# Three weight chunks at the opening of MLP, attention input and FFN: split one after another, or half by half

## The chip, the cores and the metric

The kernel runs on one core of a Trainium2 chip. The metric is device time in microseconds (us) of one execution. Three executions of the kernel before took 2520.97, 2524.18 and 2525.96 us; their median is 2524.18 us.

## What is computed

Two transformer blocks in float32, one after the other, on one sequence of 256 tokens with 2048 channels. Cut to the parts that matter here (both blocks modulate their norms by vectors made from a small input `c`):

```
# block 1: conv mixer, then an MLP
mod = silu(c) @ mod_w + mod_b                 # sh1, sc1, g1, sh2, sc2, g2
x = x + (1 + g1) * conv_mixer(rms_norm(x, norm1_g) * (1 + sc1) + sh1)
h = rms_norm(x, norm2_g) * (1 + sc2) + sh2
x = x + (1 + g2) * (square(relu(h @ mlp_w1)) @ mlp_w2)            # 2048 -> 8192 -> 2048
# block 2: two kinds of attention, then a gated FFN
h = rms_norm(x, norm1_w) * (1 + sc1) + sh1
qa, ka, va, qb, kb, vb, ga, gb = split(h @ w_in)                  # attention input
x = x + g1 * (merged_attention(...) @ w_out)
h = rms_norm(x, norm2_w) * (1 + sc2) + sh2
x = x + g2 * ((silu(h @ w_gate) * (h @ w_up)) @ w_down)           # 2048 -> 5632 -> 2048
return rms_norm(x, final_w)
```

## The kernel before

**Layout.** Activations lie channels first: 16 blocks of 128 channels on the partitions, 256 tokens along the free side. A weight matrix comes in chunks of 1 MB: 128 output channels by 2048 inputs, so a chunk is a tile `wf` of 128 x (16 x 128).

**Float32 by parts.** Each weight chunk and each activation is split into a high part (a cast to fp32r) and a low part (the remainder). A product is three matmuls per block of 128 inputs (`mm`, L189): high weight by high and by low activation, and low weight by high activation. A chunk is therefore 16 x 3 = 48 matmuls. `load_w` (L166) makes the two parts of a chunk in two halves of eight input blocks: for each half a cast by ScalarE into a tile `wh` (L177), then a subtraction by VectorE into a tile `wl` (L180). There are 4 buffers for `wf`, 4 for `wh` and 4 for `wl`, so all split halves that are alive at a time are at most four.

**Order of loads.** `weights` (L136) lists all chunks in the order of use. `take` (L160) returns the next one and always loads and splits one chunk further ahead (AHEAD = 1), so the chunk after the one in use is split before it is needed.

**The stages.** `linear` (L200) walks over the chunks of a matrix. At the opening of a stage whose activations are being made (MLP, attention input, FFN) it takes three chunks at once (`lead=3`): `mm_group` goes over the 16 input blocks and for each of them runs the matmuls of all three chunks, so that TensorE has three chunks' work for each activation block that arrives. All other chunks come one by one. Called w0, w1, w2 here are the three chunks of an opening, and w3, w4 the two that follow. The third `take` of an opening loads and splits w3.

**The norm ahead of a stage.** `norm_to` makes the activations `hHL` of a stage from `x`: for each of the 16 blocks a scaling by VectorE (L342), the high part by ScalarE (L344) and the low part by VectorE (L345). It starts when `rstd` (L302 to L307) has the reciprocal root of the sum of squares, for which TensorE adds up the squares (L327, L329). Ahead of the MLP it also needs the shift vector `SH2` of block 1. That comes from `mod_part_pe`: 16 loads `wm` of 1 MB from `mod_w` (L249), each multiplied by TensorE (L251), then a transpose (L258) and an addition (L259). The `wm` loads use the same 4 `wf` buffers as the weight chunks.

**What sets the order.** The framework's scheduler turns the program into one list for each engine before the run, and gives out the buffers of a pool in the order of the program. Each engine works through its own list. All loads are issued by SyncE (SP).

Of the kernel before, what the change touches and what calls it, by code (L numbers as in the profile page):

```python
# [10 lines left out]
F32R = mybir.dt.float32r  # L11
AF = mybir.ActivationFunctionType
ALU = mybir.AluOpType
AX = mybir.AxisListType

P = 128
D = 2048
KB = D // P
S = 256
# [31 lines left out]
QKV_ORDER = [8, 9, 10, 11, *range(8)] + [b + i for i in range(8) for b in (12, 20, 28)]  # L51
# [21 lines left out]
class Builder:  # L73
# [62 lines left out]
    def weights(self):  # L136

        a = self.a
        out = []
        for j in range(EARLY, 16):  # L140
            out += [(a["conv_in"][16 + j], 16, j not in NATIVE), (a["conv_in"][j], 16)]
        out += [(a["conv_out"][j], 16) for j in range(16)]
        for g in range(4):
            out += [(a["w1"][g * 16 + j], 16) for j in range(16)]
            out += [(a["w2"][j][:, g * D:(g + 1) * D], 16) for j in range(16)]
        out += [(a["win"][b], 16) for b in QKV_ORDER]
        out += [(a["win"][b], 16) for b in (36, 52)]
        for j in range(16):
            if j < 15:
                out += [(a["win"][b + j + 1], 16) for b in (36, 52)]  # L150
            out.append((a["oab"][j], 16))
        out += [(a["wout"][j], 16) for j in range(16)]
        f0 = 0
        for n in FF_GROUPS:
            out += [((a["wg"] if j % 2 == 0 else a["wu"])[f0 + j // 2], 16) for j in range(2 * n)]
            out += [(a["wd"][j][:, f0 * P:(f0 + n) * P], n) for j in range(16)]
            f0 += n
        return out

    def take(self):  # L160
# [2 lines left out]
            self.ahead.append(self.load_w(*self.plan.pop(0)))  # L163
        return self.ahead.pop(0)

    def load_w(self, src, nk=16, parted=True):  # L166

        w = self.wp.tile([P, nk, P], F32, tag="wf", name=self.nm("wf"))
        self.nc.sync.dma_start(out=w, in_=src.rearrange("p (k c) -> p k c", c=P))
        if not parted:  # L170
            return w
        parts = []
        for k0 in range(0, nk, 8):
            n = min(8, nk - k0)
            wh = self.sp.tile([P, n, P], F32R, tag="wh", name=self.nm("wh"))
            wl = self.sp.tile([P, n, P], F32R, tag="wl", name=self.nm("wl"))
            self.nc.scalar.copy(wh, w[:, k0:k0 + n, :])  # L177
            if self.between:
                self.between()
            self.nc.vector.tensor_tensor(out=wl, in0=w[:, k0:k0 + n, :], in1=wh, op=ALU.subtract)  # L180
            parts.append((wh, wl))
        return parts

    def mm(self, ps, w, k, x, first, last):

# [5 lines left out]
    def mm_group(self, ws, x, ks, xs=None):  # L191
# [5 lines left out]
                self.mm(ps, w, k, x[:, kx], i == 0, i == len(ks) - 1)  # L197
        return pss

    def linear(self, n, x, nk, evict, step=None, lead=3):  # L200

        j = 0
        while j < n:
            g = lead if j == 0 else 1
            g = min(g, n - j)
            ws = [self.take() for i in range(g)]
            pss = self.mm_group(ws, x, list(range(nk)))
            for i in range(g):
                evict(j + i, pss[i])
                if step:  # L210
                    step()
            j += g
# [59 lines left out]
    def step(self, n=None):  # L272
        self.due += self.rate if n is None else n
        while self.due >= 1 and self.jobs:
            self.due -= 1
            while self.jobs:
                try:
                    next(self.jobs[0])
                    break
                except StopIteration:  # L280
                    self.jobs.pop(0)
        if not self.jobs:
            self.due = 0.0
# [802 lines left out]
```

## Time and profile before

| | before |
|---|---|
| median of three executions | 2524.18 us (2520.97 to 2525.96) |
| the profiled execution | 2528.09 us |
| its span in the profile | 2526.3 us |
| TensorE busy (matmuls) | 2458.1 us, 97% |
| VectorE, ScalarE, GpSimd busy | 1680.5, 1226.7, 148.7 us |
| moved by DMA | 639.15 MB, mean 253 GB/s |

PE is TensorE's matmuls and PEld its weight loads; DVE is VectorE, ACT ScalarE, POOL GpSimd, SP SyncE. Matmuls are pipelined, so the time of one row is longer than the distance from one to the next. A row's bracket names the idle time of the engine just before it and what ended that. PEclk is the granted TensorE clock as a share of 2.4 GHz: 0.5 is 1.2 GHz.

### The profile page before, as it was taken

How to read it: one execution, taken by the hardware profiler on the slowest of the kernel's cores; microseconds unless marked ns; L12 is line 12 of the kernel's file. 1: busy time of each engine (PE TensorE's matmuls, PEld its weight loads, DVE VectorE, ACT ScalarE, POOL GpSimd, SP SyncE). 2: the span in 40 equal slices, each digit the busy share in tenths (PEclk: the TensorE clock that was granted, in tenths of full speed). 3: DMA queues.
4: the chain of work that ended last, by engine and by line, in shares of the span. 5: the costliest groups of instructions: out<-in, count | busy, mean ns of one | idle time of the engine just before them, and what ended most of it. 6: DMA issues, size and time to landing. Idle time of an engine off the chain costs nothing. (4 is left out here: it accounts for less than half of the span.)

```text
span 2526.3 us, 49401 instructions
## 1 busy us (share of the span) xinstructions
PE 2458.1 (97%) x21100; PEld 2353.7 (93%) x21100; DVE 1680.5 (67%) x2156; ACT 1226.7 (49%) x1827; POOL 148.7 (6%) x184
## 2 busy tenths in 40 slices
PE   6999899999999999999999999999999999999998
PEld 4788678899999999998999999999899999999997
DVE  3477854677777788757876667776666556566555
ACT  3366754554543544544455544444544444434443
POOL 0058900000000000000000000000000000000000
PEclk8999999999999999999999999999999999999999
DMA  9967569788787887954755577775466656665553
GB/s 397 418 237 283 215 265 332 259 306 323 272 324 286 307 326 289 330 187 168 233 193 193 198 270 271 275 290 199 167 221 237 238 206 246 213 236 207 200 181 120
DMA packets 110381, 639.15 MB, mean 253 GB/s; under 512 B 16336, under 2 KB 16592, under 8 KB 51792
## 3 DMA queue, kind: packets, MB, share of 16 engines
q1 hardware_dynamic: 110160, 635.99, 68.8%
q8 instruction: 165, 2.70, 0.4%
q14 instruction: 56, 0.46, 0.1%
HBM read 633.85 MB, written 2.10 MB: 252 GB/s over the span
## 5 line engine op out<-in xcount | busy, mean ns | idle before, releaser
L177 ACT CAST wh<-wf 128x1024 fp32r<-128x1024 f32 (+1 forms) x794 | 827.5, 1045 | 1046.9 <-PE mm L189 791.0
L189 PE MATMUL mm<-hHL,wh 128*128 128x256 f32 x7584 | 1316.5, 278 | 8.1 <-ACT hHL L344 7.7
L180 DVE TENSOR_TENSOR wl<-wf,wh 128x1024 fp32r<-128x1024 f32 (+1 forms) x794 | 965.7, 1222 | 501.7 <-ACT wh L177 497.0
L189 PEld LDWEIGHTS mm<-hHL,wh 128*128 128x128 f32 x7584 | 1151.4, 189 | 19.9 <-ACT hHL L344 9.1
L189 PE MATMUL mm<-hHL,wl 128*128 128x256 f32 x3792 | 1048.8, 277 | 2.1 <-DVE wl L180 2.1
L189 PE MATMUL mm<-uHL,wh 128*128 128x256 f32 x4480 | 768.6, 276 | 1.4 <-ACT uHL L132 0.8
L189 PEld LDWEIGHTS mm<-hHL,wl 128*128 128x128 f32 x3792 | 714.7, 188 | 3.2 <-DVE wl L180 2.9
L189 PEld LDWEIGHTS mm<-uHL,wh 128*128 128x128 f32 x4480 | 675.3, 188 | 14.6 <-ACT t L792 9.2
L189 PE MATMUL mm<-uHL,wl 128*128 128x256 f32 x2240 | 617.4, 276 | 0.0
L189 PEld LDWEIGHTS mm<-uHL,wl 128*128 128x128 f32 x2240 | 420.7, 188 | 0.9 <-issue 0.8
L230 DVE SCALAR_TENSOR_TENSOR acc<-wm,silu_c,acc 128x1024 f32<-128x1024 f32 x210 | 269.4, 1283 | 101.7 <-DMA wm<-in_w_ada_dram 77.6
L623 POOL TENSOR_TENSOR room<-room,front 128x255 f32<-128x255 f32 (+9 forms) x180 | 148.5, 826 | 169.2 <-ACT front L622 156.0
L633 DVE SCALAR_TENSOR_TENSOR mm<-room,vecs,mm 128x255 f32<-128x255 f32 (+9 forms) x180 | 84.7, 470 | 4.8
L189 PE MATMUL mm<-m,wh 128*128 128x256 f32 x512 | 87.6, 276 | 0.0
L622 ACT ACTIVATE front<-room,vecs 128x255 f32<-128x255 f32 (+9 forms) x180 | 74.9, 487 | 8.6 <-POOL room L623 8.4
L189 PEld LDWEIGHTS mm<-m,wh 128*128 128x128 f32 x512 | 77.1, 188 | 0.0
L189 PE MATMUL mm<-m,wl 128*128 128x256 f32 x256 | 70.5, 276 | 0.0
L541 PE MATMUL mm<-hHL,wh 128*128 128x256 f32 x320 | 62.4, 296 | 3.4 <-ACT hHL L132 3.4
L541 PEld LDWEIGHTS mm<-hHL,wh 128*128 128x128 f32 x320 | 52.1, 201 | 10.5 <-issue 6.7
L133 DVE TENSOR_TENSOR uHL<-t,uHL 128x256 fp32r<-128x256 f32 x124 | 51.4, 420 | 3.4 <-ACT uHL L132 3.4
L251 PE MATMUL aux<-wm,cpad 128*32 128x512 f32 x384 | 50.8, 612 | 2.8 <-DMA wm<-in_mod_w_dram 2.7
L132 ACT CAST uHL<-t 128x256 fp32r<-128x256 f32 x124 | 49.3, 403 | 4.6 <-DVE t L953 2.6
(162 smaller groups left out, 1196.0 us busy)
## 6 DMA issues: line engine op xcount, KB each, us to landing
wf<-in_w_dram SPq DMA_DIRECT2D x128, 1024.0 KB, 6.8
wm<-in_w_ada_dram SPq DMA_DIRECT2D x96, 1024.0 KB, 5.7
wf<-in_win_dram SPq DMA_DIRECT2D x68, 1024.0 KB, 5.2
wm<-in_mod_w_dram SPq DMA_DIRECT2D x64, 1024.0 KB, 6.7
wf<-in_wg_dram SPq DMA_DIRECT2D x44, 1024.0 KB, 4.8
wf<-in_wu_dram SPq DMA_DIRECT2D x44, 1024.0 KB, 4.8
wf<-in_wd_dram SPq DMA_DIRECT2D x32, 896.0 KB, 4.6
slots<-in_mod_a_dram SPq DMA_DIRECT2D x22, 1024.0 KB, 15.1
```

What stands on the lines that cost most here:

```text
L132: self.nc.scalar.copy(hi, src)
L133: self.nc.vector.tensor_tensor(out=lo, in0=src, in1=hi, op=ALU.subtract)
L177: self.nc.scalar.copy(wh, w[:, k0:k0 + n, :])
L180: self.nc.vector.tensor_tensor(out=wl, in0=w[:, k0:k0 + n, :], in1=wh, op=ALU.subtract)
L189: self.nc.tensor.matmul(ps, lhsT=a, rhs=x[:, b], start=(first and i == 0), stop=(last and i == 2))
L230: nc.vector.scalar_tensor_tensor(out=acc, in0=w[:, i], scalar=cvec[:, k + i:k + i + 1], in1=acc, op0=ALU.mult, op1=ALU.add)
L251: nc.tensor.matmul(row[32 * j:32 * j + 32, :], lhsT=cpad[:, k], rhs=w[:, j * 512:(j + 1) * 512], start=(k == 0), stop=(k == KB - 1), skip_ ...
L541: nc.tensor.matmul(dst, lhsT=w[:, c, kk], rhs=h[:, k, b], start=(k == 0 and n == 0 and half == 0), stop=(k == KB - 1 and n == 2 and half = ...
L622: nc.scalar.activation(pr, u[:, PAD:PAD + S - s], AF.Identity, scale=tap(i, j))
L623: nc.gpsimd.tensor_tensor(out=dst[:, s:], in0=dst[:, s:], in1=pr, op=ALU.add)
L633: nc.vector.scalar_tensor_tensor(out=acc[:, s:], in0=u[:, PAD:PAD + S - s], scalar=tap(i, j), in1=acc[:, s:], op0=ALU.mult, op1=ALU.add)
```

## The change

`w0`, `w1` and `w2` of the three openings are loaded without being split (a third entry in the list says so: False for them, true for all others). `linear` sees that and calls the new `by_halves`: it splits the first halves of all three chunks, runs the matmuls of input blocks 0 to 7 of all three, then does the same with the second halves. The splitting code itself moves from `load_w` into `parts`. The number of loads, casts, subtractions and matmuls stays as it was. w3 keeps its place in the list: it is loaded and split by the third `take`, ahead of `by_halves`.

```diff
         for g in range(4):
-            out += [(a["w1"][g * 16 + j], 16) for j in range(16)]
+            out += [(a["w1"][g * 16 + j], 16, g > 0 or j > 2) for j in range(16)]
             out += [(a["w2"][j][:, g * D:(g + 1) * D], 16) for j in range(16)]
-        out += [(a["win"][b], 16) for b in QKV_ORDER]
+        out += [(a["win"][b], 16, i > 2) for i, b in enumerate(QKV_ORDER)]
...
-            out += [((a["wg"] if j % 2 == 0 else a["wu"])[f0 + j // 2], 16) for j in range(2 * n)]
+            out += [((a["wg"] if j % 2 == 0 else a["wu"])[f0 + j // 2], 16, f0 > 0 or j > 2) for j in range(2 * n)]
...
+    def parts(self, w, k0, n):
+
+        wh = self.sp.tile([P, n, P], F32R, tag="wh", name=self.nm("wh"))
+        wl = self.sp.tile([P, n, P], F32R, tag="wl", name=self.nm("wl"))
+        self.nc.scalar.copy(wh, w[:, k0:k0 + n, :])
+        if self.between:
+            self.between()
+        self.nc.vector.tensor_tensor(out=wl, in0=w[:, k0:k0 + n, :], in1=wh, op=ALU.subtract)
+        return wh, wl
...
     def load_w(self, src, nk=16, parted=True):
...
         if not parted:
             return w
-        parts = []
-        for k0 in range(0, nk, 8):
-            n = min(8, nk - k0)
...
-            parts.append((wh, wl))
-        return parts
+        return [self.parts(w, k0, min(8, nk - k0)) for k0 in range(0, nk, 8)]
...
+    def by_halves(self, ws, x):
+
+        pss = [self.mmps()[:, :S] for _ in ws]
+        for k0 in (0, 8):
+            halves = [self.parts(w, k0, 8) for w in ws]
+            for k in range(k0, k0 + 8):
+                for ps, part in zip(pss, halves):
+                    self.mm(ps, {k // 8: part}, k, x[:, k], k == 0, k == KB - 1)
+        return pss
+
     def linear(self, n, x, nk, evict, step=None, lead=3):
...
             ws = [self.take() for i in range(g)]
-            pss = self.mm_group(ws, x, list(range(nk)))
+            if g > 1 and not isinstance(ws[0], list):
+                pss = self.by_halves(ws, x)
+            else:
+                pss = self.mm_group(ws, x, list(range(nk)))
```

What the change moves on the engines, at three places. In the list of the changed kernel the lines stand some further down: the cast is L170, the subtraction L173, the activation of the norm L357 (L344 before), the load of a chunk L179 (L169), of `wm` L262 (L249), the matmul still L189.

**Order 1, ScalarE at the opening of the MLP.** Before, w0 is `wf_4488` and w1 `wf_4671`; the rows run from the end of the conv output to the first activation of the norm, and the first cast of w1 comes after eight activations:

```order
L177 CAST wh_4490<-wf_4488 128x1024
L323 ACTIVATE t_466_4478<-x 128x256
L177 CAST wh_4494<-wf_4488 128x1024
L792 ACTIVATE t_474_4547<-mm_4498,vecs 128x256
L323 ACTIVATE t_475_4550<-x 128x256
L302 ACT_TABLE_LOAD
L302 ACTIVATE t_485_4595<-aux_3417,eps 128x256
L255 COPY t_481_4583<-aux_3835 128x512
L344 ACTIVATE hHL_4593<-t_488_4603,mods 128x256
```

In the change w0 is `wf_4488`, w1 `wf_4663`, w2 `wf_4665` and w3 `wf_4667`; the first two rows here are the 13th and the 14th activation of the norm:

```order
L357 ACTIVATE hHL_4585<-t_496_4643,mods 128x256
L357 ACTIVATE hHL_4585<-t_497_4647,mods 128x256
L170 CAST wh_4669<-wf_4667 128x1024
L170 CAST wh_4673<-wf_4667 128x1024
L357 ACTIVATE hHL_4585<-t_498_4651,mods 128x256
L357 ACTIVATE hHL_4585<-t_499_4655,mods 128x256
L170 CAST wh_4680<-wf_4488 128x1024
L170 CAST wh_4684<-wf_4663 128x1024
L170 CAST wh_4688<-wf_4665 128x1024
L170 CAST wh_4764<-wf_4488 128x1024
```

The two casts of w0 stood ahead of the norm; now its first cast stands behind all 16 activations and both casts of w3.

**Order 2, SyncE's loads ahead of the MLP, with the engines and load queues that each waits for.** Before (w0, five pieces of `mod_w` for `SH2`, w1, w2, w3):

```order
L169 DMA wf_4488<-in_w_dram 128x2048 [waits DMAHW3_49,DVE_49]
L249 DMA wm_4553<-in_mod_w_dram 128x2048 [waits DMAHW4_49,PE_49]
L249 DMA wm_4559<-in_mod_w_dram 128x2048 [waits DMAHW5_49,DVE_49]
L249 DMA wm_4565<-in_mod_w_dram 128x2048 [waits DMAHW6_49,PE_49]
L249 DMA wm_4571<-in_mod_w_dram 128x2048 [waits DMAHW7_49,DVE_49]
L249 DMA wm_4577<-in_mod_w_dram 128x2048 [waits DMAHW0_49,PE_49]
L169 DMA wf_4671<-in_w_dram 128x2048 [waits DMAHW1_49,PE_49]
L169 DMA wf_4681<-in_w_dram 128x2048 [waits DMAHW2_49,PE_49]
L169 DMA wf_4691<-in_w_dram 128x2048 [waits DMAHW3_49,PE_49]
```

In the change:

```order
L179 DMA wf_4488<-in_w_dram 128x2048 [waits DMAHW3_49,DVE_49]
L262 DMA wm_4545<-in_mod_w_dram 128x2048 [waits DMAHW4_49,PE_49]
L262 DMA wm_4551<-in_mod_w_dram 128x2048 [waits DMAHW5_49,DVE_49]
L262 DMA wm_4557<-in_mod_w_dram 128x2048 [waits DMAHW6_49,PE_49]
L262 DMA wm_4563<-in_mod_w_dram 128x2048 [waits DMAHW0_49,PE_49]
L262 DMA wm_4569<-in_mod_w_dram 128x2048 [waits DMAHW1_49,PE_49]
L179 DMA wf_4663<-in_w_dram 128x2048 [waits DMAHW2_49,PE_49]
L179 DMA wf_4665<-in_w_dram 128x2048 [waits DMAHW3_49,PE_49]
L179 DMA wf_4667<-in_w_dram 128x2048 [waits DMAHW7_49,DMAHW4_49,PE_49]
```

The order of the loads is the same, but the fourth piece of `mod_w`, which waited for VectorE (it got w0's buffer after the split), now waits for TensorE, and what follows moves one buffer on.

**Order 3, ScalarE and TensorE at the opening of the FFN.** ScalarE before, from w0 (`wf_20194`) and w1 (`wf_20336`) to the first activation of the norm:

```order
L177 CAST wh_20196<-wf_20194 128x1024
L177 CAST wh_20200<-wf_20194 128x1024
L323 ACTIVATE t_2478_20190<-x 128x256
L177 CAST wh_20338<-wf_20336 128x1024
L177 CAST wh_20342<-wf_20336 128x1024
L323 ACTIVATE t_2485_20254<-x 128x256
L302 ACTIVATE t_2488_20261<-aux_19248,eps 128x256
L344 ACTIVATE hHL_20259<-t_2491_20269,mods 128x256
```

In the change, with w3 `wf_20332`, w0 `wf_20194` and w1 `wf_20328`:

```order
L336 ACTIVATE t_2478_20190<-x 128x256
L170 CAST wh_20334<-wf_20332 128x1024
L170 CAST wh_20338<-wf_20332 128x1024
L170 CAST wh_20345<-wf_20194 128x1024
L170 CAST wh_20349<-wf_20328 128x1024
L336 ACTIVATE t_2481_20246<-x 128x256
L315 ACTIVATE t_2484_20253<-aux_19248,eps 128x256
L357 ACTIVATE hHL_20251<-t_2487_20261,mods 128x256
```

TensorE in the change, behind the 48 matmuls of the first halves of w0 and w1 (`mm_20344` is the result of w2, `mm_20531` that of w3):

```order
L189 MATMUL mm_20343<-hHL_20251,wh_20349 128x256 x2
L189 MATMUL mm_20343<-hHL_20251,wl_20350 128x256
L189 MATMUL mm_20344<-hHL_20251,wh_20353 128x256 x2
L189 MATMUL mm_20531<-hHL_20251,wh_20334 128x256 x2
L189 MATMUL mm_20531<-hHL_20251,wl_20335 128x256
```

The four split halves that lie ready when the norm starts were both of w0 and both of w1; now they are both of w3 and the first of w0 and of w1. The first half of w2 comes after the first half of w0 is used up, in both. The attention input's opening moves in the same way.

## Rows read from the trace of the kernel before

**Rows 1.** The page: span, and busy time of each engine.
```profile
span 2526.3 us, 49401 instructions
PE 2458.1 (97%) x21100; PEld 2353.7 (93%) x21100; DVE 1680.5 (67%) x2156; ACT 1226.7 (49%) x1827; POOL 148.7 (6%) x184
```

**Rows 2.** Busy time by stretch: from:to, length, busy us (x instructions), PEclk, DMA share, GB/s.
```profile
400.00:500.00 100.00, 95.17 (x754) 81.39 (x751) 56.59 (x87) 47.61 (x79) 0.00 (x0) 0.95 0.82 294
900.00:1000.00 100.00, 100.00 (x885) 100.00 (x884) 82.34 (x96) 41.30 (x43) 0.00 (x0) 1.00 0.82 305
1100.00:1200.00 100.00, 95.49 (x800) 93.11 (x798) 66.84 (x99) 46.32 (x68) 0.00 (x0) 0.98 0.51 178
```

**Rows 3.** TensorE's timeline at the MLP's opening: start, us, engine, line, op, tiles, count [idle].
```profile
454.88 1.93 PE L251 MATMUL aux<-wm,cpad 128*32 128x512 f32 x8 [2.22 <-DMA wm<-in_mod_w_dram]
459.44 1.10 PE L189 MATMUL mm<-hHL,wh 128*128 128x256 f32 x2 [0.81 <-ACT hHL L344]
460.34 0.42 PE L189 MATMUL mm<-hHL,wl 128*128 128x256 f32 x1
460.99 0.41 PE L189 MATMUL mm<-hHL,wl 128*128 128x256 f32 x1
```

**Rows 4.** L189 alone, by stretch: PE busy (x), PEld busy (x), PEclk, DMA share, GB/s.
```profile
459.00:486.50 27.50, 25.96 (x191) 24.92 (x192) 0.89 0.57 196
1789.30:1814.00 24.70, 24.55 (x193) 23.86 (x194) 0.93 0.28 97
```

**Rows 5.** SyncE's timeline ahead of the MLP.
```profile
444.41 0.33 SPq L249 DMA_DIRECT2D wm<-in_mod_w_dram  x1
448.55 0.33 SPq L249 DMA_DIRECT2D wm<-in_mod_w_dram  x1
451.00 0.33 SPq L169 DMA_DIRECT2D wf<-in_w_dram  x1
```

**Rows 6.** Loads from issue to landing: wm at 440 to 460, wf at 1755 to 1800, wf at 445 to 470.
```profile
DMA to landing us min/median/max: 6.2/6.3/6.7
DMA to landing us min/median/max: 4.7/4.8/4.9
DMA to landing us min/median/max: 6.3/8.1/9.5
```

**Rows 7.** VectorE's timeline at the MLP's opening.
```profile
443.17 1.22 DVE L180 TENSOR_TENSOR wl<-wf,wh 128x1024 fp32r<-128x1024 f32 x1
459.43 0.89 DVE L345 SCALAR_TENSOR_TENSOR hHL<-t,mods,hHL 128x256 fp32r<-128x256 f32 x2 [0.58 <-ACT hHL L344]
460.62 2.46 DVE L345 SCALAR_TENSOR_TENSOR hHL<-t,mods,hHL 128x256 fp32r<-128x256 f32 x6
```

**Rows 8.** ScalarE's timeline at the MLP's opening.
```profile
458.88 3.30 ACT L344 ACTIVATE hHL<-t,mods 128x256 fp32r<-128x256 f32 x8 [1.42 <-DVE mods L259]
462.09 1.98 ACT L177 CAST wh<-wf 128x1024 fp32r<-128x1024 f32 x2
```

**Rows 9.** TensorE's clock on its way up, in the MLP and in the FFN (columns as in rows 2).
```profile
464.00:466.00 2.00, 2.00 (x13) 1.80 (x12) 2.00 (x6) 2.00 (x7) 0.00 (x0) 0.77 0.55 87
1792.00:1794.00 2.00, 2.00 (x16) 2.00 (x16) 2.00 (x6) 0.93 (x4) 0.00 (x0) 0.82 0.00 0
```

**Rows 10.** The FFN's opening: TensorE, its weight loads, ScalarE.
```profile
1789.38 1.23 PE L189 MATMUL mm<-hHL,wh 128*128 128x256 f32 x3 [3.33 <-ACT hHL L344]
1797.54 0.59 PEld L189 LDWEIGHTS mm<-hHL,wh 128*128 128x128 f32 x3 [0.25 <-ACT wh L177]
1796.43 1.05 ACT L177 CAST wh<-wf 128x1024 fp32r<-128x1024 f32 x1 [1.55 <-issue]
```

**Rows 11.** The attention input's opening: SyncE, VectorE.
```profile
1175.30 0.39 SPq L225 DMA_DIRECT2D wm<-in_w_ada_dram  x1
1192.76 0.75 DVE L228 TENSOR_SCALAR acc<-wm,silu_c 128x1024 f32<-128x1024 f32 x1
1203.84 1.22 DVE L180 TENSOR_TENSOR wl<-wf,wh 128x1024 fp32r<-128x1024 f32 x1
```

More of the change, by code (lines that the diff above doesn't have):

```diff
@@ L171, in load_w @@
             return w
-        parts = []
-        for k0 in range(0, nk, 8):
-            n = min(8, nk - k0)
[L175 to L180, printed above, removed]
-            parts.append((wh, wl))
-        return parts
+        return [self.parts(w, k0, min(8, nk - k0)) for k0 in range(0, nk, 8)]
     def mm(self, ps, w, k, x, first, last):
```

## The prediction

> **What bounds the kernel.** The busy times come first: TensorE works 2458.1 of 2526.3 us, no other engine more than 67% of them, so TensorE sets the time [rows 1]. The stretches then say where it stands still. In the middle of a stage it is busy 100.00 of 100 us at full clock, a matmul every 100/885 = 0.113 us; around the MLP's opening it loses 4.8 us and around the attention input's 4.5 [rows 2]. So whatever starts TensorE later at an opening and isn't made up in that opening is paid in full. TensorE's own timeline gives the MLP's opening: after the transposes of `SH2` it waits only 0.81 us, for the first activation `hHL`, and starts at 459.44 [rows 3]. 191 matmuls are done by 486.50, so the 192 of w0 to w3 by about 486.55: 27.1 us where 192 x 0.113 = 21.7 are needed [rows 4]. The 5.4 us lost are mostly the low clock: at 459.44 the granted clock is half and becomes full at about 465.0 (the stretch from 464 to 466 has 0.77, which is 0.92 us at 0.5) [rows 9]. The FFN's opening waits 3.33 us for the norm, starts at 1789.38 [rows 10] and has its 192 matmuls in some 24.5 us, a loss of 2.85 [rows 4]; its clock is full again 3.3 us after the start [rows 9].
>
> **The change in the MLP, step 1: the buffers.** Before, w0 is split before the norm and its `wf` buffer is free when VectorE ends the second subtraction (443.17 + 1.22 = 444.4) [rows 7]; SyncE issues the fourth piece of `mod_w` at 444.41 and the fifth at 448.55, when TensorE gives back another, then w1 at 451.00 [rows 5]. Now w0 keeps its buffer. The fourth piece waits for TensorE until 448.55, the fifth until 451.00, and w1 to w3 are queued behind them on SyncE, The last piece is thus issued 2.45 us later. TensorE waits for this piece: its last eight matmuls start at 454.88, after 2.22 us idle for that DMA [rows 3]. Landing took 6.3 us there, 4.7 to 4.9 where a load was alone, up to 6.7 at worst [rows 6]. With 4.7 the last piece is late by D = 2.45 + 4.7 - 6.3 = 0.85, with 6.7 by 2.85. I take **D = 2.0**: near the 2.45 of an equal landing, as the same pieces are the nearest row, and a little under it, as one transfer fewer runs beside it. (The Trainium skill, "DMA: Bandwidth & Descriptors", section "Latency and other measured facts", says that a lighter load on the memory makes the fixed cost of a transfer smaller; by it D would be nearer 0.85 and the sum below about 10.9 us. The 4.8 us of the lone loads agree.)
>
> **Step 2: who stands ahead of the first matmul.** The third `take` loads and splits w3 before the first halves of w0 to w2 are split. So w3 gets two of the four `wh` and two of the four `wl` buffers, and ScalarE's and VectorE's lists have its parts first: 14 activations, two casts of w3, two activations, and only then the first cast of w0. Before, both casts of w0 were over ahead of the norm. On VectorE the 14th scaled block is the 18th of the operations that start at 459.43 (0.40 us apart, from six L345 in 2.46 us); 459.43 + 18 x 0.40 = 466.65, and with the activation behind it 467.2 [rows 7, 8]. Two casts of w3 take 1.98 us [rows 8]: 469.15. w3 gets the last piece's buffer, given back at 454.88 + 1.93 + D = 458.8 [rows 3], and lands at 466.9 with the median of 8.1 us, at 468.3 with the 9.5 of the worst [rows 6]; the 14th activation ends at 467.2 + D = 469.2, so w3 is there. The last two activations (0.40 each, from eight in 3.30) end at 470.0 [rows 8], w0's first cast (1.05, the FFN's row [rows 10]) at 471.05. With D all of it is 2.0 us later: TensorE's first matmul on `hHL` at **473.05** in place of 459.44, that is **13.6 us** later.
>
> **Step 3: what comes back in the opening.** All 16 activations are ready by then, so no block is waited for. VectorE subtracts in the order w3, two L345, w3, w0 (1.22 and 0.41 us each [rows 7]), which ends 1.9 us after the first matmul; TensorE can place 4 matmuls until then. At half clock a matmul comes every 0.217 us (three from 460.34 to 460.99 [rows 3]); with 5.5 us at half clock as before, the remaining 3.6 us hold 17. The other 171 run at 0.113: 19.3 us. At the change from w0's first half to the third chunk's TensorE waits for w2's cast, since w3 holds its buffers: 1.05 less four matmuls, 0.65, and 0.1 at the second halves. Together 1.9 + 3.6 + 19.3 + 0.75 = 25.6 us, so the 192nd matmul ends at 473.05 + 25.6 = 498.6 against 486.55: **+12.0 us**. 5.5 us of low clock is the nearest row, in the same place; the other end is the FFN's 3.3, which gives 2.2 x (1 - 0.113/0.217), about 1.0 us less; as TensorE is thinly used in its first 1.9 us, 2 us of low clock more (1.0 us of time) is the end above. (The Trainium skill, "TensorE: Matmul & The Clock Gate", section "What's actually happening", has the clock set by how busy the array was recently, not by a count of matmuls; a start with few matmuls would so keep it low for longer than 5.5 us, and the sum would be up to 1.0 us higher. No row here shows such a thin start.) Nothing later gives these microseconds back: behind the opening TensorE is at 100.00 of 100 us [rows 2].
>
> **Attention input and FFN.** There the three or four first casts fit ahead of the norm, since w3 is on the chip long before: a lone load takes 4.8 us [rows 6]. TensorE still starts on the first `hHL`, and the norm's wait of 3.33 us [rows 10] stays. The 48 matmuls of w0's and w1's first halves run, then TensorE waits 0.65 us for w2's cast (1.05 less four matmuls), as against a wait of 0.25 us for the same chunk before [rows 10]; w3's matmuls fill in. I take **0 for each**, between -0.25 (that wait vanishes) and +1.0 (the whole cast lies bare). In the attention input the piece `wm` issued at 1175.30 now waits for w0's buffer, until some 1193, and VectorE, which used it at 1192.76, waits for it to 1193 + 6.3 = 1199. Behind it on VectorE stand subtractions of the next chunks, one at 1203.84 among them [rows 11]; four 1.22 us subtractions end by 1204, so it costs 0, at most the +1.0. GpSimd's list is untouched, and the numbers of casts, loads and matmuls stay, so there is no other term.
>
> **Sum.** 12.0 + 0 + 0. The profiled execution took 2528.09 us, so 2540.1 on its scale; the median of the runs, 2524.18, stands 3.9 us lower: **2536.2 us**. A measurement here can tell some 0.2%, 5.05 us, from no change.
>
> **The rivals.**
> *More (+14.5 to +18).* w3's load becomes the gate. It does so when it lands over 10.4 us after 458.8, that is behind the 14th activation. For it: four loads leave in a row there, and 9.5 has been seen in that stretch [rows 6]. Against: the median is 8.1. With D = 2.85, 1.0 us of longer low clock, 1 us in each other opening and 1 us for w3, 12.0 + 0.85 + 1.0 + 2 + 1 = 16.85 us.
> *Less (+7 to +9.5).* D = 0.85, the clock up after 3.3 us, no waits: 12.0 - 1.15 - 1.0 - 0.75 = 9.1; if TensorE lost nothing at all behind its first matmul, 13.6 - 1.15 - 5.4 = 7.05. For it: the lone loads and the FFN's clock. Against: the same place showed 6.3 and 5.5.
> *No slower.* The loss in the MLP is paid back by one mechanism: w3's split halves, which now lie ready before the norm of attention input and FFN, give TensorE work on each block without a wait and at full clock right from the first `hHL`. Both openings would then lose nothing: 2 x 2.85 = 5.7 us regained, and with the MLP at its floor the change is 7.05 - 5.7 = +1.4 us, 2521.7 to 2527 us, no difference that can be told. It decides if the matmuls of the FFN's opening come at 0.113 us from the start. Against it: most of the 2.85 us is the low clock, which follows the 3.33 us wait [rows 9, 10], and the change does not touch that wait.
> *The change does not do what it says.* That is in the forecast: w3 stands ahead of the first halves and takes half of the split buffers, so the third chunk's half waits for w0's first half to be used up. If w3's parting were put behind after all (by the lists it isn't), TensorE would start after w0's cast without the two casts of w3 and the change would cost about 2 us less, inside the range.
>
> **How the numbers follow.** The forecast, +9.5 to +14.5 us, has a chance of 0.72: its steps are counts from the lists and durations of the same place. More has 0.12, less 0.12, no slower 0.04. The range should leave out no more than 2 in 10: from +7.8 to +16.8 us, 2532.0 to 2541.0 us, which takes in both ends of D and of the low clock. Slower by over 0.2% is all but the last rival: 0.95, with 0.04 for within 0.2% and 0.01 for faster.
>
> **What the profile after would show.** In the MLP the first matmul on `hHL` (L189) at about 473, with about 12 us idle before it ended by ScalarE's cast; on ScalarE the casts of w3 between the 14th and the 15th activation; two `wm` loads issued at about 448.6 and 451.0; the granted clock at half until about 478.5; the 192nd matmul at about 498.6. In the FFN the wait of 3.3 us and the loss of 2.85 as before. A first matmul on `hHL` in the MLP before 464.4 (under 5 us late) would make the forecast wrong, as would a matmul rate in the two other openings without loss.

## Result and profile after

The changed kernel is **slower**: ratio 1.0075 (95% interval 1.0061 to 1.0088), that is +15.4 to +22 us on the 2522.97 us of the kernel before. Its executions took 2540.19, 2541.44 and 2544.28 us; a fourth took 6413.38 us, a disturbance that the ratio leaves out but that raises the median of the four to 2542.86 us. The same kernel, run again beside a tighter set, gave 2538.92 us and 1.0063 (1.0049 to 1.0077). The forecast was +12.0 us, 2536.2 us, range 2532.0 to 2541.0: the sign and the main place are right, but the amount is 6.9 us short of the first timing (+18.9) and 3.9 us short of the second (+15.9).

The profiled execution took 2540.19 us. First the page, beside [rows 1]:

```profile
span 2538.2 us, 49395 instructions
PE 2454.9 (97%) x21100; PEld 2350.0 (93%) x21100; DVE 1681.8 (66%) x2156; ACT 1228.8 (48%) x1827; POOL 148.8 (6%) x184
```

Every engine executes as many instructions of work as before. TensorE is busy for about as long (2454.9 us, before 2458.1), so it stands still for longer. Next comes TensorE's timeline at the MLP's opening, beside [rows 3] (L342 is the sum of squares, L264 the pieces of `mod_w`, L271 the transposes). Before, the matmuls that end the sum of squares stand here:

```profile
449.26 0.70 PE L329 MATMUL aux<-t,ones_d 128*128 128x256 f32 x2
```

In the change:

```profile
448.12 0.70 PE L342 MATMUL aux<-t,ones_d 128*128 128x256 f32 x2
448.75 1.92 PE L264 MATMUL aux<-wm,cpad 128*32 128x512 f32 x14
452.44 1.06 PE L264 MATMUL aux<-wm,cpad 128*32 128x512 f32 x8 [1.78 <-DMA wm<-in_mod_w_dram]
456.23 1.49 PE L264 MATMUL aux<-wm,cpad 128*32 128x512 f32 x8 [2.72 <-DMA wm<-in_mod_w_dram]
458.41 1.11 PE L271 MATMUL aux<-const,t 128*128 128x128 f32 x4 [0.69 <-ACT t L268]
471.77 0.79 PE L189 MATMUL mm<-hHL,wh 128*128 128x256 f32 x2 [12.25 <-ACT wh L170]
472.72 0.80 PE L189 MATMUL mm<-hHL,wh 128*128 128x256 f32 x2 [0.15 <-ACT wh L170]
473.77 0.58 PE L189 MATMUL mm<-hHL,wl 128*128 128x256 f32 x1 [0.25 <-DVE wl L173]
```

Where TensorE waited 0.81 us for an activation, it now waits 12.25 us for a cast of a weight, and then for VectorE's low part. ScalarE says which casts came first, beside [rows 8]:

```profile
459.77 3.31 ACT L357 ACTIVATE hHL<-t,mods 128x256 fp32r<-128x256 f32 x8 [1.41 <-DVE mods L272]
464.40 1.31 ACT L357 ACTIVATE hHL<-t,mods 128x256 fp32r<-128x256 f32 x3 [1.32 <-DVE t L355]
466.78 1.31 ACT L357 ACTIVATE hHL<-t,mods 128x256 fp32r<-128x256 f32 x3 [1.06 <-DVE t L355]
467.99 1.98 ACT L170 CAST wh<-wf 128x1024 fp32r<-128x1024 f32 x2
469.88 0.91 ACT L357 ACTIVATE hHL<-t,mods 128x256 fp32r<-128x256 f32 x2
470.69 1.98 ACT L170 CAST wh<-wf 128x1024 fp32r<-128x1024 f32 x2
```

The two casts at 467.99 are w3's, the first of the two at 470.69 is w0's, and TensorE begins 1.08 us after it starts. SyncE, beside [rows 5]:

```profile
447.41 2.77 SPq L262 DMA_DIRECT2D wm<-in_mod_w_dram  x2
450.71 3.18 SPq L179 DMA_DIRECT2D wf<-in_w_dram  x2
```

The last piece leaves at 447.41 + 2.77 - 0.33 = 449.85, 1.73 us behind the last square; before it left at 448.55, 0.71 us ahead of it. The 192 matmuls are all done by 498.70, beside [rows 4]:

```profile
471.00:498.70 27.70, 25.81 (x192) 24.60 (x193) 0.89 0.44 152
```

In the attention input and the FFN the wait for the norm stays as in [rows 10], and one new wait for w2's cast appears in each:

```profile
1187.10 1.23 PE L189 MATMUL mm<-hHL,wh 128*128 128x256 f32 x3 [3.34 <-ACT hHL L357]
1195.29 0.74 PE L189 MATMUL mm<-hHL,wh 128*128 128x256 f32 x4 [0.73 <-ACT wh L170]
...
1799.03 1.23 PE L189 MATMUL mm<-hHL,wh 128*128 128x256 f32 x3 [3.34 <-ACT hHL L357]
1808.43 0.74 PE L189 MATMUL mm<-hHL,wh 128*128 128x256 f32 x4 [0.73 <-ACT wh L170]
```

The matmul that ends a sum of squares (L329 before, L342 after), the first near 15 us and then one ahead of the MLP, of attention input, of the FFN and of the end, divides a trace into four stretches that can be compared between kernels (us; "start" is from the square ahead of the MLP to the first matmul on `hHL`):

| trace | to MLP | MLP | of it start | attention | FFN | profiled execution |
|---|---|---|---|---|---|---|
| before, first | 433.42 | 725.03 | 10.18 | 611.06 | 728.80 | 2528.09 |
| changed, first | 433.14 | 734.94 | 23.65 | 611.94 | 731.08 | 2540.19 |

In this pair the MLP lost 9.9 us, attention 0.9, the FFN 2.3. That is 13.1, and the executions differ by 12.1; but the two timings give 15.9 and 18.9. So the experiments had two questions: which step costs what, and why the pair of traces shows less than the timings.

### The profile page after: what moved, and what is told of

Its sections match the earlier page's. It is cut to its first block, busy times and chain, and to the rows that moved or that the text cites. A ratio compares the mean times of both kernels' runs of the same rounds, so it can differ in the third digit from the quotient of the medians.

```text
span 2538.2 us, 49395 instructions
## 1 busy us (share of the span) xinstructions
PE 2454.9 (97%) x21100; PEld 2350.0 (93%) x21100; DVE 1681.8 (66%) x2156; ACT 1228.8 (48%) x1827; POOL 148.8 (6%) x184
## 4 chain that ended last, share of the span: by engine, by line
PE 92%; DMA 5%; DVE 2%; ACT 1%; issue 0%; POOL 0%; SPq 0%; POOLq 0%; DVEq 0%; ACTq 0%
PE mm L189 84%; DMA front<-in_mod_a_dram 2%; DMA slots<-in_mod_a_dram 2%; PE aux L264 1%; PE mm L554 1%; DMA wm<-in_mod_w_dram 1%; PE mm L620 1%; PE mm L734 1%; PE aux L402 1%; PE aux L434 1%; PE aux L249 0%; ACT front L635 0%; PE aux L765 0%; DVE wl L173 0%; ACT wh L170 0%
## 5 line engine op out<-in xcount | busy, mean ns | idle before, releaser
L189 PE MATMUL mm<-hHL,wh 128*128 128x256 f32 x7584 | 1316.1, 278 | 21.2 <-ACT wh L170 14.5
L170 ACT CAST wh<-wf 128x1024 fp32r<-128x1024 f32 (+1 forms) x794 | 828.0, 1047 | 1039.7 <-PE mm L189 777.4
L173 DVE TENSOR_TENSOR wl<-wf,wh 128x1024 fp32r<-128x1024 f32 (+1 forms) x794 | 965.9, 1223 | 511.7 <-ACT wh L170 508.7
L189 PEld LDWEIGHTS mm<-hHL,wh 128*128 128x128 f32 x7584 | 1151.2, 189 | 33.2 <-ACT wh L170 16.2
L189 PE MATMUL mm<-hHL,wl 128*128 128x256 f32 x3792 | 1047.0, 277 | 0.2 <-DVE wl L173 0.2
L189 PE MATMUL mm<-uHL,wh 128*128 128x256 f32 x4480 | 768.2, 276 | 1.1 <-ACT uHL L132 0.9
L189 PEld LDWEIGHTS mm<-hHL,wl 128*128 128x128 f32 x3792 | 714.3, 188 | 1.2 <-DVE wl L173 0.5
L189 PEld LDWEIGHTS mm<-uHL,wh 128*128 128x128 f32 x4480 | 675.4, 188 | 14.1 <-ACT t L805 9.2
L189 PE MATMUL mm<-uHL,wl 128*128 128x256 f32 x2240 | 616.4, 275 | 0.0
L189 PEld LDWEIGHTS mm<-uHL,wl 128*128 128x128 f32 x2240 | 420.5, 188 | 0.9 <-issue 0.8
L189 PE MATMUL mm<-m,wh 128*128 128x256 f32 x512 | 87.6, 276 | 0.0
L189 PEld LDWEIGHTS mm<-m,wh 128*128 128x128 f32 x512 | 77.1, 188 | 0.0
L189 PE MATMUL mm<-m,wl 128*128 128x256 f32 x256 | 70.4, 275 | 0.0
L264 PE MATMUL aux<-wm,cpad 128*32 128x512 f32 x384 | 50.5, 607 | 5.4 <-DMA wm<-in_mod_w_dram 5.3
## 6 DMA issues: line engine op xcount, KB each, us to landing
slots<-in_mod_a_dram SPq DMA_DIRECT2D x22, 1024.0 KB, 15.9
```

What stands on the lines that cost most here:

```text
L189: self.nc.tensor.matmul(ps, lhsT=a, rhs=x[:, b], start=(first and i == 0), stop=(last and i == 2))
L264: nc.tensor.matmul(row[32 * j:32 * j + 32, :], lhsT=cpad[:, k], rhs=w[:, j * 512:(j + 1) * 512], start=(k == 0), stop=(k == KB - 1), skip_ ...
```

## Experiments

Theory: in the MLP, w3's parts ahead of w0's and w0's kept buffer cost the time. Rivals: the halves themselves; the two other openings; or the one trace of before was an odd one.

### Both kernels again

No edit; `a_again` is the changed kernel, `b_again`, `b_look2` and `b_look3` are the kernel before.

> The changed kernel once more, for a tighter ratio and a second trace. Theory: the loss is the late first matmul of the MLP (13.5 us in its own frame, of which up to 3.5 come back), the two other openings add 1 to 3 us by the length of the low clock, which differs from run to run; then the ratio is 1.005 to 1.006 (+12 to +15 us) once both kernels are run often enough. Rival: a further systematic loss of about 5 us that the first trace does not show; then the ratio stays at 1.007 or more. In the trace the theory has the first matmul on hHL in the MLP 12 to 13.5 us later than before, counted from the last square of the conv output.

> The kernel before once more. Its first profiled execution (2528.09 us) lies above all its timed ones (2520.97 to 2525.96). If that execution was a slow one by chance, this trace has a shorter span (2519 to 2524 us) and lacks some of its small losses: the low clock in the first 100 us (0.91 there), TensorE's waits for VectorE's low parts between 540 and 900 us (3 us together), or a longer low clock at an opening. If those losses are fixed, they are all there again. The ratio must be 1.000 within 0.001.

> The kernel before, a third trace of it. It tells how the distance from the last square of the conv output to the first matmul on hHL is spread in this kernel (10.18 and 7.63 us so far), and how often VectorE's low parts keep TensorE waiting later in the MLP (3 us in the first trace, 0.2 in the second). If the first trace was the odd one, this one is near 7.6 us and its segment from that square to the one ahead of the attention input near 720 us, not 725.

> The kernel before, a fourth trace, for the spread of the distance from the last square to the MLP's first matmul (10.18, 7.63 and 13.32 us so far) and of the low clock behind it (5.4, 3.4 and 5.8 us).

| trace | to MLP | MLP | of it start | attention | FFN | profiled execution |
|---|---|---|---|---|---|---|
| `a_again` | 431.50 | 736.46 | 24.07 | 612.50 | 729.73 | 2538.92 |
| `b_again` | 432.65 | 720.13 | 7.63 | 611.26 | 728.98 | 2521.67 |
| `b_look2` | 433.15 | 725.28 | 13.32 | 610.90 | 728.77 | 2526.33 |
| `b_look3` | 432.59 | 719.93 | 7.61 | 611.11 | 728.82 | 2521.07 |

`a_again` has 1.0063 (1.0049 to 1.0077), between what theory and rival expected; `b_again` 0.9996 (0.9988 to 1.0005). The four traces of the kernel before differ in the MLP by 5.3 us and nowhere else by more than 0.9. TensorE's timelines of `b_again` and of `b_look2` show where:

```profile
447.38 0.70 PE L329 MATMUL aux<-t,ones_d 128*128 128x256 f32 x2
...
451.77 1.06 PE L251 MATMUL aux<-wm,cpad 128*32 128x512 f32 x8 [0.99 <-DMA wm<-in_mod_w_dram]
...
455.01 1.10 PE L189 MATMUL mm<-hHL,wh 128*128 128x256 f32 x2 [0.81 <-ACT hHL L344]
```

```profile
447.43 0.70 PE L329 MATMUL aux<-t,ones_d 128*128 128x256 f32 x2
...
456.19 1.94 PE L251 MATMUL aux<-wm,cpad 128*32 128x512 f32 x8 [5.35 <-DMA wm<-in_mod_w_dram]
...
460.75 1.10 PE L189 MATMUL mm<-hHL,wh 128*128 128x256 f32 x2 [0.81 <-ACT hHL L344]
```

In both, the last piece of `mod_w` is issued 0.71 us ahead of the square (446.67 and 446.72), and it lands 5.1 and 9.4 us later. So the MLP's start in the kernel before hangs on one load whose landing is spread over 4.4 us (5.0 in `b_look3`, 6.3 in the first trace). A late landing costs more than its own delay, since the last eight matmuls then run at half clock (1.94 us in `b_look2`, 1.06 in `b_again`). The changed kernel's start hardly varies: 23.65 and 24.07, behind a landing of 6.3 us in both. The first trace of before was a late one of four, not the odd one: two are near 7.6, two at 10 and more. It also had small waits of TensorE for VectorE's low parts between 500 and 900 us, 1.8 us in the view of waits, that `b_again` has not (0.2).

The means of four and of two traces differ by 735.70 - 722.59 = +13.1 us in the MLP, +1.1 in attention, +1.6 in the FFN and -0.6 ahead of the MLP: +15.2 us, close to the second timing (1.0063, +15.9 us).

### `b_hold`: step 1 alone

```diff
             ws = [self.take() for i in range(g)]
+            if self.hold:
+                self.hold = False
+                self.nc.vector.tensor_tensor(out=self.small(1), in0=self.raw[-4][:, 0, 0:1], in1=x[:, KB - 1, 1, 0:1], op=ALU.add)
```

(`raw` collects the `wf` tiles, so `raw[-4]` is w0; `hold` is set once, ahead of the MLP.)

> The kernel before, with one added VectorE operation of one column behind the norm that reads w0 of the MLP, so that w0 keeps its buffer as in the changed kernel and the loads leave in the same order and with the same waits; the splits stay where they were. It prices step 1 alone. Theory: the last piece of mod_w leaves 2.45 us later and lands 6.3 us after that, where the undisturbed kernel has 5.1 to 6.3, so the first matmul on hHL comes 10.2 to 12.7 us after the last square of the conv output (10.18 and 7.63 in the two traces of before, 12.66 with w3 split late); ratio 1.001 to 1.002, +2.5 to +5 us. Rival (the kept buffer costs nothing, the later loads are hidden): ratio 1.000, first matmul at 7.6 to 10.2 us.

Measured: 1.0016 (1.0007 to 1.0025), start 12.53 us, MLP 725.6 us. The theory holds. The loads leave as in the changed kernel, and TensorE's timeline shows the late piece (the sum of squares is L334 here):

```profile
447.62 0.70 PE L334 MATMUL aux<-t,ones_d 128*128 128x256 f32 x2
...
455.59 1.94 PE L256 MATMUL aux<-wm,cpad 128*32 128x512 f32 x8 [2.78 <-DMA wm<-in_mod_w_dram]
...
460.15 1.10 PE L191 MATMUL mm<-hHL,wh 128*128 128x256 f32 x2 [0.81 <-ACT hHL L349]
```

Keeping w0's buffer costs 0.7 to 2.5 thousandths, 1.8 to 6.3 us; in the MLP's stretch it is 725.6 - 722.6 = 3.0 us against the mean of before. The start of this one trace lies within the spread of before (7.6 to 13.3 us), so it is the timing that shows the cost.

### `w3_late`: w3 behind the halves

```diff
-            out += [(a["w1"][g * 16 + j], 16, g > 0 or j > 2) for j in range(16)]
+            out += [(a["w1"][g * 16 + j], 16, g > 0 or j > 3) for j in range(16)]
...
                 pss = self.by_halves(ws, x)
+                self.ahead[0] = [self.parts(self.ahead[0], k0, 8) for k0 in (0, 8)]
```

(The same for attention input and FFN.)

> As the changed kernel, but w3 is loaded unsplit and split behind the halves of w0 to w2 at all three openings. Theory (w3's two casts and its hold on half of the split buffers cost the MLP's late start): the first matmul on hHL in the MLP comes with the first activation again, only D = 2.0 to 2.5 us later than before, and the ratio falls to 1.000 to 1.002. Rival (the halves themselves, or w0's buffer kept longer, cost it): the ratio stays above 1.004.

Measured: 1.0025 (1.0015 to 1.0036), 2530.36 us, MLP 728.84 us. The start is as expected, 12.66 us after the square, the same as `b_hold`'s. The ratio is a little over what was expected. Two other waits come up in TensorE's timeline, 3.3 us together, and behind the first of them the granted clock is 0.50 again (468.4 to 475.2):

```profile
459.50 1.10 PE L189 MATMUL mm<-hHL,wh 128*128 128x256 f32 x2 [0.81 <-ACT hHL L358]
467.12 0.50 PE L189 MATMUL mm<-hHL,wh 128*128 128x256 f32 x2 [1.43 <-ACT wh L170]
469.47 0.58 PE L189 MATMUL mm<-hHL,wl 128*128 128x256 f32 x1 [1.85 <-DVE wl L173]
```

The first halves of w1 and w2 are split late, since VectorE's list has w1's low part behind 13 and w2's behind all 16 activations. The MLP's stretch so goes up in three steps: 722.6 (before), 725.6 (buffer kept), 728.8 (split by halves, w3 behind), 735.7 (w3 ahead). The last one, 6.9 us, is w3's place alone; by the timings it is 2538.92 - 2530.36 = 8.6 us, with the two other openings in it.

### `mlp_only` and `qkv_ffn_only`

`mlp_only` has the third entry (split later) in the list for the MLP alone, `qkv_ffn_only` for the two others alone:

```diff
-        out += [(a["win"][b], 16, i > 2) for i, b in enumerate(QKV_ORDER)]
+        out += [(a["win"][b], 16) for b in QKV_ORDER]
```

(This is the line of the attention input in `mlp_only`, which changes that of the FFN in the same way; `qkv_ffn_only` changes that of the MLP instead.)

> Halves in the MLP's opening alone; attention input and FFN as before. Theory: nearly the whole loss is here, ratio 1.004 to 1.006, and the changed kernel is slower than this one by 0 to 3 us. Rival (attention input and FFN carry a real part): the changed kernel is slower than this one by 4 us or more.

> Halves in attention input and FFN, the MLP as before. The segments between last squares of the traces so far give +0.7 to +1.3 us for attention input and +0.7 to +2.2 for the FFN. Theory: ratio 1.0004 to 1.0012, +1 to +3 us, from one wait of 0.73 us for w2's cast at each opening and from the low clock, whose length differs between runs. Rival (nothing at all, as predicted): ratio within 0.0004 of 1.

Measured: `mlp_only` 1.0061 (1.0048 to 1.0074), 0.3 us under `a_again`; `qkv_ffn_only` 1.0006 (0.9997 to 1.0015). Nearly all of the loss is the MLP's. In the trace of `qkv_ffn_only` attention takes 613.2 and the FFN 730.0 us, 2.1 and 1.2 over the mean of before, with the new wait of 0.73 us in each; the timing alone can't tell this from nothing. Part of it is not the change but the clock. `mlp_only` has these two openings as they were before, and its stretches are longer as well. The granted clock below is the mean over 10 us from the first matmul of the opening:

| trace | opening | attention: clock, stretch | FFN: clock, stretch |
|---|---|---|---|
| before, first | as before | 0.83, 611.06 | 0.83, 728.80 |
| `mlp_only` | as before | 0.69, 612.19 | 0.76, 729.46 |
| changed, first | by halves | 0.83, 611.94 | 0.70, 731.08 |
| `a_again` | by halves | 0.76, 612.50 | 0.84, 729.73 |
| `qkv_ffn_only` | by halves | 0.70, 613.20 | 0.83, 729.99 |

The attention rows of `mlp_only` and `qkv_ffn_only` (columns as in [rows 2]):

```profile
1190.20:1200.20 10.00, 9.89 (x57) 9.44 (x57) 8.29 (x22) 5.03 (x12) 0.00 (x0) 0.69 0.14 57
1173.00:1183.00 10.00, 9.20 (x52) 8.86 (x53) 8.31 (x22) 5.04 (x12) 0.00 (x0) 0.70 0.01 2
```

At like clock an opening by halves is longer by 0.9 to 1.2 us: 611.94 against 611.06 and 613.20 against 612.19 in attention, 729.73 and 729.99 against 728.80 in the FFN.

### `b_pace`, `a_pace`, `w0_whole`, `w0_pace`: the late piece taken out, and a version with w0 whole

```diff
-WOUT_PACE = 1.2
+WOUT_PACE = 1.45
```

`b_pace` is the kernel before, `a_pace` the changed one with this edit. In `w0_whole` only w1 and w2 are split by halves, and w3 behind them; `w0_pace` has both:

```diff
-            halves = [self.parts(w, k0, 8) for w in ws]
+            halves = [w[k0 // 8] if isinstance(w, list) else self.parts(w, k0, 8) for w in ws]
```

> The kernel before with WOUT_PACE 1.45 in place of 1.2: the pieces of mod_w for SH2 are spread faster over the conv output, so that one and not five of them are left to the end. If the late last piece is what sets the MLP's start in the kernel before (7.4 to 13.3 us after the last square in five traces), the first matmul comes with the norm, 4.5 to 6 us after the last square, the spread of that distance is gone, and the ratio is 0.9975 to 0.9990. Rival: the faster loads delay the conv output's chunks (DMA share is 0.9 there already) by as much, ratio 0.999 to 1.002.

> The changed kernel with the same faster pace. The last piece of mod_w is early and w0's kept buffer costs nothing, so step 1 is out; what is left is w3 ahead of w0 on ScalarE. ScalarE's list has w3's first cast behind 6 activations and w0's first cast behind 9 and both of w3's. Theory: the first matmul waits for w3 to land and the casts, 14 to 18 us after the last square (23.65 and 24.07 with the slow pace), the ratio to the undisturbed kernel 1.002 to 1.004, still 3 us or more behind b_pace's. Rival (the late mod_w pieces made most of it): first matmul under 10 us after the square and the time within 1 us of b_pace's.

> At all three openings w0 is split whole ahead of the norm as before, only w1 and w2 by halves, and w3 is split behind them: the four split buffers then hold w0's two halves and the first halves of w1 and w2. w0's buffer is free early again, so D is 0 and the first matmul of the MLP comes with the first activation, 7.6 to 10.2 us after the last square. If the third chunk's first half being ready saves TensorE's waits at the openings, the ratio is 0.9990 to 0.9998; if those waits were nothing, it is 1.000; if w1's second half, which now waits for a buffer, is late, 1.0005 to 1.0015.

> w0 whole, w1 and w2 by halves, w3 split behind them, with the faster pace. If halves of w1 and w2 are worth anything once the activations come early, it is 0.5 to 1.5 us faster than b_pace; if nothing, equal to it within 0.5 us.

| kernel | ratio | to MLP | MLP | of it start |
|---|---|---|---|---|
| `b_pace` | 1.0002 (0.9993 to 1.0010) | 438.33 | 716.12 | 7.05 |
| `a_pace` | 1.0076 (1.0064 to 1.0089) | 440.50 | 731.79 | 12.46 |
| `w0_whole` | 0.9999 (0.9990 to 1.0008) | 432.80 | 720.98 | 7.40 |
| `w0_pace` | 1.0006 (0.9997 to 1.0015) | 440.46 | 718.48 | 6.05 |

`b_pace`: the start is 7.05 us, and the MLP gains 6.5 us against the mean of before, but the stretch ahead of it loses 5.4; no gain, as its rival had it. `a_pace` was expected at 1.002 to 1.004 and is 1.0076: **with the late piece gone the loss is not smaller**. Against `b_pace` it is 2542.36 - 2525.37 = 17.0 us. TensorE's timeline shows why the first matmul alone misleads:

```profile
455.13 0.70 PE L342 MATMUL aux<-t,ones_d 128*128 128x256 f32 x2 [0.54 <-ACT t L336]
467.59 0.80 PE L189 MATMUL mm<-hHL,wh 128*128 128x256 f32 x2 [11.33 <-ACT wh L170]
470.54 0.80 PE L189 MATMUL mm<-hHL,wh 128*128 128x256 f32 x2 [2.15 <-ACT wh L170]
475.30 0.58 PE L189 MATMUL mm<-hHL,wl 128*128 128x256 f32 x1 [3.96 <-DVE wl L173]
```

It starts at 467.59 and stops after two matmuls and again after two more: the steady work begins at 475.30, 20.2 us after the square, when VectorE has subtracted w0's low part. Its timeline in `a_pace`, behind the row of ScalarE's casts of w3's second half and w0's first:

```profile
465.56 1.98 ACT L170 CAST wh<-wf 128x1024 fp32r<-128x1024 f32 x2
...
470.17 0.88 DVE L355 SCALAR_TENSOR_TENSOR t<-x,a,t 128x256 f32<-128x256 f32 x2
470.96 1.22 DVE L173 TENSOR_TENSOR wl<-wf,wh 128x1024 fp32r<-128x1024 f32 x1
472.10 0.88 DVE L358 SCALAR_TENSOR_TENSOR hHL<-t,mods,hHL 128x256 fp32r<-128x256 f32 x2
472.89 3.49 DVE L173 TENSOR_TENSOR wl<-wf,wh 128x1024 fp32r<-128x1024 f32 x3
```

w3's first low part at 470.96, the last two activations, w3's second, and only then w0's, though w0's cast was over by 467.54 (465.56 + 1.98). So with the faster pace the start is set by VectorE's list as much as by ScalarE's. Against the slow pace the steady work begins 5.4 us earlier behind the square (473.77 - 448.12 = 25.65 there), but `b_pace` gains as much in its MLP (6.5 us).

`w0_whole` has the start of the kernel before (0.76 us of wait for the last piece) and its time, so halves of w1 and w2 are worth nothing that the timing shows; `w0_pace` is not faster than `b_pace`. No version beats the kernel before.

## Why the prediction was right or wrong

**Right: the mechanism and its place.** The first matmul was foretold 473.05 - 449.26 = 23.8 us after the last square; it came after 23.65 and 24.07. The wait of 12.25 us is ended by ScalarE's cast, w3's casts stand between the 14th and the 15th activation, and w3 was on the chip in time. The rival without effect fell: no loss came back in the other openings, where the 3.34 us wait stayed. The second timing (+15.9) and the traces (+15.2) lie in the band of the rival "more", but not by its mechanism: ScalarE didn't wait for w3's load ahead of 467.99. The first timing (+18.9) lies above that band.

**Step 1: right; the size of D by luck.** The last piece left 1.73 + 0.71 = 2.44 us later, as worked out (2.45). It landed 6.38 us after its issue (TensorE's 456.23 less 449.85), not sooner for the lighter load: so the piece was 2.5 us late in the first pair, where 2.0 was taken and 2.45 was the value of an equal landing. The norm still began only 2.0 us later (first activation 11.65 us behind the square, before 9.62), since the last eight matmuls happened to take 1.49 us in place of 1.93. By the Trainium skill's rule of a smaller fixed cost under a lighter load ("DMA: Bandwidth & Descriptors", "Latency and other measured facts") the prediction had D nearer 0.85. Four traces with the changed order of loads (both of the changed kernel, `b_hold`, `w3_late`) have 6.2 to 6.4 us, so they don't agree.

**Step 2: right as a size.** 13.6 us against 23.65 - 10.18 = 13.47 in the first pair. What failed is the other side of the difference. The 10.18 us of the one trace of before were taken as that kernel's own; four traces give 7.61, 7.63, 10.18 and 13.32, mean 9.7. Against the mean the step is 14.2 us.

**Step 3: too much came back.** The 192 matmuls were put at 25.6 us from the first and took 26.9 (471.77 to 498.70), hardly less than the 27.1 of [rows 4]. In this trace the clock was as assumed (mean 0.89 in both). TensorE waited 0.15 + 0.25 us at the start, 0.68 for w2's cast and lost some 0.45 us where it went over to new halves (9 matmuls in each of the us from 486 and from 491, 11 beside them); the rest of the 1.3 us is not placed. In `a_again` they took 28.0 us (470.16 to 498.20). There the clock was at half for 7.7 us from the first matmul, where 5.5 us were assumed and 2 us more stood at the end of the range (columns as in [rows 4]):

```profile
470.16:477.90 7.74, 7.33 (x31) 6.74 (x32) 0.50 0.39 135
```

The reading that the assumption came from was wrong too. The prediction put the 5.4 us that the opening of before loses mostly down to the low clock. `b_look3` had full clock throughout, and in as long a stretch around its first matmul it did 190 of these matmuls, where the first trace did 191 (first line of [rows 4]); `b_again` and `b_look2` did 190 as well, at a mean clock of 0.94 and 0.89:

```profile
454.46:481.96 27.50, 24.41 (x190) 23.00 (x191) 1.00 0.67 231
```

TensorE's waits there for activations and low parts come to 2.5 us, in the first trace to 1.1. So in the kernel before TensorE is held back by what the norm and the splits deliver, and the low clock costs its opening nothing. In the changed kernel all activations are ready, and the low clock is paid. In the whole MLP 13.1 us were lost against the mean of before, where 12.0 were forecast.

**Attention input and FFN: the two zeros were wrong.** "I take **0 for each**, between -0.25 (that wait vanishes) and +1.0 (the whole cast lies bare)" is the step that failed most clearly. The wait for w2's cast came as worked out (0.73 us, 0.65 foretold), but before has no wait at TensorE in these openings behind the first matmul, so nothing was to be set against it; the 0.25 us of [rows 10] is a wait of the weight load, which didn't stop the matmuls. At like clock each opening costs 0.9 to 1.2 us, the upper bound of the term: some 2 us that the sum of 12.0 lacks. The means over all traces differ by 1.1 and 1.6 us; there the clock's own spread is in it, which `mlp_only` shows with untouched openings.

**The subtraction of 3.9 us.** The forecast took 3.9 us off, as the profiled execution lay over the median, and left +12.0 as it was. That is right for an excess that has nothing to do with the place that changes. Here much of it lay in the MLP's opening, which started 2.5 us later than in the two early traces, and in the small waits behind it (1.8 us): the 12.0 were worked out against a late start. Why the last piece of `mod_w` lands so steadily in the changed kernel (6.3 us in both traces) is open. On its own scale the forecast was 2540.1 us, and the profiled execution took 2540.19. That agreement is luck: in this pair the MLP lost 9.9 us where 12.0 were forecast, and the two other stages 3.2 us where nothing was.

So the effect is about +15 to +16 us by both sets of traces and the second timing, of which 12.0 was forecast; the recorded +18.9 us is at the upper side of that and its interval (from +15.4) still holds it. What share of the last 3 us between the two timings is chance can't be told from four executions.

## What to carry to other kernels

Before a forecast is made against one trace, ask of the place that the change rewrites whether this execution was typical there: a wait that one load ends can be spread (over 4.4 us here), and a difference between profile and median mustn't be carried over if the change removes what caused it. When weights are loaded ahead but split later, look at who splits next: a lookahead that takes its buffers first turns "in halves" into "last", and this shows in the lists of ScalarE and VectorE before any run. The first matmul of a stage says little when the second waits too; compare stretches between fixed points, and at like clock. A low clock beside a loss need not be its cause: here the loss stayed in an execution at full clock.

## What the runs showed of the hardware

A load of 1 MB in the same place of the same kernel landed after 5.0, 5.1, 6.3 and 9.4 us in four executions. TensorE's clock at the same opening is as little fixed: the granted clock between 450 and 480 us was 1.00 in `b_look3`, 0.94 in `b_again` and 0.77 in `b_look2`, as these rows show in this order (busy time, matmuls, granted clock, DMA share, GB/s):

```profile
450.00:480.00 30.00, 24.86 (x191) 1.00 0.74 269
```

```profile
450.00:480.00 30.00, 25.65 (x190) 0.94 0.75 270
```

```profile
450.00:480.00 30.00, 22.04 (x142) 0.77 0.65 236
```

TensorE had waited 0.97, 0.99 and 5.35 us for the last piece in them. It is no strict order: in `qkv_ffn_only` a wait of 2.94 us left the clock full over the first 8 us from the first matmul. The MLP's opening of before takes the same time at any of these clocks, as step 3 above shows. In the FFN's opening the same wait of 3.3 us was followed by full clock at about 1792.7 before ([rows 9]), 3.3 us after the start, and at about 1805.0 after, 6.0 us after it:

```profile
1804.00:1806.00 2.00, 2.00 (x15) 2.00 (x15) 2.00 (x6) 0.54 (x2) 0.00 (x0) 0.75 0.04 8
```

The change touches neither that wait nor the matmuls right behind it, and `mlp_only`, with the FFN's opening of before, had its clock at half for 4.8 us from the first matmul. So the 2.7 us are the clock's own spread, some 1.3 us of time at 0.217 and 0.113 us a matmul.

The Trainium skill ("TensorE: Matmul & The Clock Gate", "What's actually happening") has the clock follow how busy the array was of late. By that rule the prediction had a thin start keep the clock low for longer than 5.5 us. The changed MLP's first trace doesn't show it (5.4 us at half from the first matmul), but `a_again` (7.7), `mlp_only` (7.3) and `a_pace` (13.9) agree; in `a_pace` TensorE did four matmuls in its first 7.7 us.
